# A 16 x 512-byte load on SP's queue ahead of the first large load of an Lp-pooling kernel

## The chip, the cores and the metric

The kernel runs on one core of a Trainium2 chip. The metric is the device time of one execution in microseconds; the number of record is the median of three runs. Profiles come from one execution of their own, recorded by the hardware profiler.

## The reference

The input x is float32, 32 x 256 x 4096; p is 2 and kernel_size is 4. Each output is the root of the mean of the squares of four neighbours:

```python
for i in range(out_length):                      # out_length = length // kernel_size
    start = i * kernel_size
    end = start + kernel_size
    window = np.abs(x[:, :, start:end]) ** p
    result[:, :, i] = (np.mean(window, axis=-1)) ** (1.0 / p)
```

So 134.2 MB are read, 33.6 MB are written, and each element is used once.

## The kernel before

x is taken as one flat array, and so is the output. The work is cut into 20 pieces, each of 128 partitions by up to 13,184 floats (52,736 bytes in a partition, 6.6 MB in all). Pieces form six blocks (L51): four of four pieces, then pieces 18, 16 and 17, then piece 19 alone. Within a block each partition holds one contiguous stretch of x.

There are three tiles for pieces of x, xt0 to xt2 (`X_SLOTS`, L43); piece i goes to tile i modulo 3. The tile `ot` holds four pieces' results, and a tile `st` in PSUM takes the sums of pieces 4, 8, 12 and 16. A tile `first` of one column serves a square root of a constant at the start (L129).

The steps of a piece:
- `load(i)` (L79 to L83): SP issues a DMA from x to the tile, in SP's queue.
- `square` (L88, L89): ACT squares the tile in place.
- `pairs` (L91 to L95) and `fours` (L97 to L99): DVE adds the squares in two steps, to a quarter of the length.
- `roots` (L106, with `root` in L102): ACT takes the square root with a scale of 1/4, for one piece or several neighbouring ones.
- `store(b, queue)` (L85, L86): a block of results goes out, blocks 0 to 2 from ACT's queue, blocks 3 to 5 from SP's.

The order is written by hand (`manual_schedule`, L62): each engine carries out its instructions in the order of the program text. Loads 0 to 2 are issued first (L122, L123). From then on load i + 3 is issued after the sums of piece i (L144, L145), since it overwrites the same tile; SP waits there for DVE. The last three pieces are treated apart (L147 to L172): DVE takes over part of the squares of pieces 18 and 19, and the last two blocks are stored separately.

Each DMA adds to a semaphore when it has landed. The DMAs of the program take eight such semaphores in turn.

The part that the change touches is the place just ahead of L122, before anything has been issued on SP, and the list of tiles in L58 to L61.

Of the kernel before, what the change touches and what calls it, by code (L numbers as in the profile page):

```python
# [1 line left out]

# [4 lines left out]


@with_exitstack
def kernel(  # L10
    ctx: ExitStack,
    tc: tile.TileContext,
    x: bass.AP,
    p: float,
    kernel_size: int,
    out: bass.AP,
):

    nc = tc.nc

    assert float(p) == 2.0, "kernel specialized for p == 2"
    k = int(kernel_size)  # L30
    assert k == 4, "kernel specialized for kernel_size == 4"

    P = nc.NUM_PARTITIONS
    fp32 = mybir.dt.float32
    Act = mybir.ActivationFunctionType
    add = mybir.AluOpType.add
    xf = x.rearrange("b c l -> (b c l)")
    of = out.rearrange("b c l -> (b c l)")
    total = xf.shape[0] // P

    W = 13184
    R = W // k
    X_SLOTS = 3  # L43
    NARROW = W - 32
    LAST = total - 18 * W - NARROW
    widths = [W] * 3 + [NARROW] + [W] * 15 + [LAST]
    n = len(widths)
    assert 0 < LAST <= W and LAST % 16 == 0


    blocks = [[0, 1, 2, 3], [4, 5, 6, 7], [8, 9, 10, 11], [12, 13, 14, 15], [18, 16, 17], [19]]  # L51
    block_of = {i: b for b, group in enumerate(blocks) for i in group}
    block_width = [sum(widths[i] for i in group) for group in blocks]

    x_pool = ctx.enter_context(tc.tile_pool(name="x_pool", bufs=1))
    o_pool = ctx.enter_context(tc.tile_pool(name="o_pool", bufs=1))
    s_pool = ctx.enter_context(tc.tile_pool(name="s_pool", bufs=1, space=bass.MemoryType.PSUM))
    x_tiles = [x_pool.tile([P, W], fp32, name=f"xt{j}") for j in range(X_SLOTS)]  # L58
    o_tile = o_pool.tile([P, 4 * R], fp32, name="ot")
    first = o_pool.tile([P, 1], fp32, name="first")  # L60
    s_tile = s_pool.tile([P, 4096], fp32, name="st")  # L61
    ctx.enter_context(tc.manual_schedule())  # L62

    def rows(flat, b, div):
        at = sum(block_width[:b]) * P // div
        return flat[at:at + block_width[b] * P // div].rearrange("(p w) -> p w", p=P)


    free = x_tiles[17 % X_SLOTS]
    place = {i: o_tile[:, i % 4 * R:i % 4 * R + widths[i] // k] for i in range(16)}  # L70
    place[18] = free[:, R:2 * R]
    place[19] = free[:, 0:LAST // k]
    place[16] = free[:, 2 * R:3 * R]
    place[17] = free[:, 3 * R:4 * R]
    held = [o_tile[:, 0:w // k] for w in block_width[:4]] + [free[:, R:4 * R], place[19]]

    xs, loads, stores, sums, squares = {}, {}, {}, {}, {}

    def load(i):  # L79
        b = block_of[i]  # L80
        at = sum(widths[j] for j in blocks[b][:blocks[b].index(i)])
        xs[i] = x_tiles[i % X_SLOTS][:, 0:widths[i]]
        loads[i] = nc.sync.dma_start(out=xs[i], in_=rows(xf, b, 1)[:, at:at + widths[i]])  # L83

    def store(b, queue):  # L85
        stores[b] = queue.dma_start(out=rows(of, b, k), in_=held[b])  # L86

    def square(v):  # L88
        return nc.scalar.activation(out=v, in_=v, func=Act.Square)  # L89

    def pairs(v):  # L91

        q = v.rearrange("p (n j) -> p n j", j=k)
        h = v[:, 0:v.shape[1] // 2].rearrange("p (n j) -> p n j", j=2)
        return nc.vector.tensor_tensor(out=h, in0=q[:, :, 0:2], in1=q[:, :, 2:4], op=add)  # L95

    def fours(o, v):  # L97
        h = v[:, 0:v.shape[1] // 2].rearrange("p (n j) -> p n j", j=2)
        return nc.vector.tensor_tensor(out=o, in0=h[:, :, 0], in1=h[:, :, 1], op=add)  # L99

    def root(o, s):
        return nc.scalar.activation(out=o, in_=s, func=Act.Sqrt, scale=1.0 / k)  # L102

    summed = {i: s_tile[:, 0:R] if i in (4, 8, 12, 16) else place[i] for i in range(n)}

    def roots(*group):  # L106
        if len(group) == 1:
            root(place[group[0]], summed[group[0]])
        else:
            v = o_tile[:, group[0] % 4 * R:(group[-1] % 4 + 1) * R]  # L110
            r = root(v, v)
            if group[0] in (5, 9):

                implied(r, stores[block_of[group[0]] - 1])
        if group[-1] in (3, 7, 11):
            store(block_of[group[-1]], nc.scalar)

    def implied(later, earlier):

        tc.declare_no_dep(later.ins, earlier.ins, reason="implied by the other waits")  # L120

    for i in range(X_SLOTS):  # L122
        load(i)  # L123


    ahead = {4: (3,), 8: (7,), 12: (11,)}
    behind = {3: [(0, 1, 2)], 7: [(5, 6), (4,)], 11: [(9, 10), (8,)], 14: [(12,)], 15: [(13, 14)], 16: [(15,)]}

    root(first[:, :], nc.const_aps.tensor(1.0, (P, 1), fp32))  # L129
    for i in range(17):  # L130
        if i in ahead:
            roots(*ahead[i])
        s = square(xs[i])
        squares[i] = s
        if i == 3:
            implied(s, squares[0])
        if i in (3, 7, 11):

            for earlier in sums[i - X_SLOTS]:
                implied(s, earlier)  # L140
        for group in behind.get(i, []):
            roots(*group)
        sums[i] = pairs(xs[i]), fours(summed[i], xs[i])
        if i + X_SLOTS < n:  # L144
            load(i + X_SLOTS)  # L145

    store(3, nc.sync)  # L147
    square(xs[17])
    pairs(xs[17])
    fours(summed[17], xs[17])  # L150
    later = {18: 4608, 19: 2000}

    def shared_square(i):
        v = xs[i][:, 0:later[i]]
        nc.vector.tensor_tensor(out=v, in0=v, in1=v, op=mybir.AluOpType.mult)  # L155
        square(xs[i][:, later[i]:widths[i]])

    def shared_pairs(i):
        implied(pairs(xs[i]), loads[i])

    shared_square(18)
    roots(16)
    roots(17)
    shared_pairs(18)
    fours(summed[18], xs[18])
    shared_square(19)
    roots(18)
    store(4, nc.sync)
    shared_pairs(19)
    fours(summed[19], xs[19])  # L170
    roots(19)
    store(5, nc.sync)  # L172


# [1 line left out]
_INS = ['x', 'p', 'kernel_size']  # L176
_OUTS = [((32, 256, 1024), 'float32')]

_NUMBERS = {'p': 2.0, 'kernel_size': 4}


# [26 lines left out]
```

## Time and profile before

| | |
|---|---|
| median of 3 runs | 394.06 us (393.84 to 394.38) |
| span of the profiled execution, first to last instruction | 392.3 us |
| median less that span | 1.8 us |
| ACT busy | 274.4 us (70%), 37 instructions |
| DVE busy | 218.2 us (56%), 42 instructions |
| GpSimd busy | 0.2 us, 4 instructions |
| HBM read and written | 134.22 MB and 33.55 MB |
| mean rate over the span | 428 GB/s |

Times inside the execution count from its first instruction. The profile names engines ACT (ScalarE), DVE (VectorE), POOL (GpSimd) and SP (SyncE); "SPq" is the issue of DMAs by SP and "ACTq" that by ACT. A row such as `xt<-in_x_dram` is what an instruction writes and reads, and L83 is a line of the kernel. A transfer is cut into packets, which 16 DMA engines carry; the packet records give the start, the duration and the size of each. The profiled execution's own time beyond its span isn't recorded; the median of the runs stands beside it.

### The profile page before, as it was taken

How to read it: one execution, taken by the hardware profiler on the slowest of the kernel's cores; microseconds unless marked ns; L12 is line 12 of the kernel's file. 1: busy time of each engine (PE TensorE's matmuls, PEld its weight loads, DVE VectorE, ACT ScalarE, POOL GpSimd, SP SyncE). 2: the span in 40 equal slices, each digit the busy share in tenths (PEclk: the TensorE clock that was granted, in tenths of full speed). 3: DMA queues.
4: the chain of work that ended last, by engine and by line, in shares of the span. 5: the costliest groups of instructions: out<-in, count | busy, mean ns of one | idle time of the engine just before them, and what ended most of it. 6: DMA issues, size and time to landing. Idle time of an engine off the chain costs nothing.

```text
span 392.3 us, 176 instructions
## 1 busy us (share of the span) xinstructions
DVE 218.2 (56%) x42; ACT 274.4 (70%) x37; POOL 0.2 (0%) x4
## 2 busy tenths in 40 slices
DVE  0009477580693274905942748069418485699970
ACT  1095695979950859799509597995098999969910
POOL 0000000000000000000000000000000000000000
DMA  8999999999999999999999999999999999999997
GB/s 344 430 430 430 430 440 435 452 457 366 430 430 430 430 430 430 430 441 446 452 446 441 436 430 436 430 430 430 430 430 430 430 430 430 430 453 415 430 413 342
DMA packets 3744, 167.77 MB, mean 428 GB/s; under 512 B 416, under 2 KB 416, under 8 KB 416
## 3 DMA queue, kind: packets, MB, share of 16 engines
q1 hardware_dynamic: 3312, 147.53, 87.4%
q10 hardware_dynamic: 432, 20.25, 11.9%
HBM read 134.22 MB, written 33.55 MB: 428 GB/s over the span
## 4 chain that ended last, share of the span: by engine, by line
DMA 43%; ACT 30%; DVE 23%; issue 0%; ACTq 0%; SPq 0%; DVEq 0%
DMA xt<-in_x_dram 43%; ACT xt L89 28%; DVE xt L95 14%; DVE ot L99 5%; DVE xt L99 3%; DVE xt L155 2%; ACT ot L102 2%; ACT xt L102 1%; ACTq L86 0%; SPq L83 0%; DVEq L95 0%
## 5 line engine op out<-in xcount | busy, mean ns | idle before, releaser
L89 ACT ACTIVATE xt<-xt 128x13184 f32<-128x13184 f32 (+3 forms) x20 | 216.7, 10847 | 92.3 <-DMA xt<-in_x_dram 91.0
L95 DVE TENSOR_TENSOR xt<-xt 128x6592 f32<-128x6592 f32 (+2 forms) x20 | 139.7, 6985 | 144.1 <-ACT xt L89 143.9
L99 DVE TENSOR_TENSOR ot<-xt 128x3296 f32<-128x3296 f32 (+1 forms) x13 | 46.7, 3592 | 17.9 <-DMA out_dram<-ot 17.6
L102 ACT ACTIVATE ot<-ot 128x6592 f32<-128x6592 f32 (+3 forms) x8 | 37.2, 4655 | 7.0 <-DVE ot L99 7.0
L102 ACT ACTIVATE xt<-xt 128x3296 f32<-128x3296 f32 (+1 forms) x3 | 8.5, 2836 | 8.8 <-DVE xt L99 8.8
L99 DVE TENSOR_TENSOR st<-xt 128x3296 f32<-128x3296 f32 x4 | 14.4, 3600 | 0.1
L99 DVE TENSOR_TENSOR xt<-xt 128x3296 f32<-128x3296 f32 (+1 forms) x3 | 10.4, 3461 | 0.1
L102 ACT ACTIVATE ot<-st 128x3296 f32<-128x3296 f32 x3 | 8.7, 2898 | 0.0
L155 DVE TENSOR_TENSOR xt<-xt 128x4608 f32<-128x4608 f32 (+1 forms) x2 | 7.2, 3593 | 0.0
L102 ACT ACTIVATE xt<-st 128x3296 f32<-128x3296 f32 x1 | 2.9, 2898 | 0.0
L102 ACT ACT_TABLE_LOAD x1 | 1.3, 1283 | 0.7 <-PEq L189 0.7
L102 ACT ACTIVATE first<-const-float32-1.0 128x1 f32<-128x1 f32 x1 | 0.2, 202 | 0.0
L189 POOL MEMSET const-bfloat16-1.0<- 128x1 bf16 x1 | 0.1, 101 | 0.0
L189 POOL MEMSET const-uint8-127<- 128x1 uint8 x1 | 0.1, 101 | 0.0
L189 POOL MEMSET const-float32-0.0<- 128x1 f32 x1 | 0.1, 98 | 0.2 <-issue 0.2
L189 POOL MEMSET const-float32-1.0<- 128x1 f32 x1 | 0.1, 98 | 0.0
## 6 DMA issues: line engine op xcount, KB each, us to landing
xt<-in_x_dram SPq DMA_DIRECT2D x18, 6592.0 KB, 29.8
out_dram<-ot ACTq DMA_DIRECT2D x2, 6592.0 KB, 35.1
out_dram<-ot SPq DMA_DIRECT2D x1, 6592.0 KB, 37.1
out_dram<-ot ACTq DMA_DIRECT2D x1, 6588.0 KB, 36.3
xt<-in_x_dram SPq DMA_DIRECT2D x1, 6576.0 KB, 24.7
xt<-in_x_dram SPq DMA_DIRECT2D x1, 5840.0 KB, 21.9
out_dram<-xt SPq DMA_DIRECT2D x1, 4944.0 KB, 16.1
out_dram<-xt SPq DMA_DIRECT2D x1, 1460.0 KB, 8.2
```

Source lines behind the costliest of these rows:

```text
L89: return nc.scalar.activation(out=v, in_=v, func=Act.Square)
L95: return nc.vector.tensor_tensor(out=h, in0=q[:, :, 0:2], in1=q[:, :, 2:4], op=add)
L99: return nc.vector.tensor_tensor(out=o, in0=h[:, :, 0], in1=h[:, :, 1], op=add)
L102: return nc.scalar.activation(out=o, in_=s, func=Act.Sqrt, scale=1.0 / k)
L155: nc.vector.tensor_tensor(out=v, in0=v, in1=v, op=mybir.AluOpType.mult)
L189: nc = _bacc.Bacc("TRN2", target_bir_lowering=False, num_devices=1)
```

## The change

One tile is added, 16 partitions of 128 floats, and one DMA into it, issued on SP ahead of the three large loads. Its source is x seen as 16 equal rows, of which the first 128 floats each are read; neighbouring rows are 8 MiB apart. Nothing in the kernel reads the tile.

```diff
     s_tile = s_pool.tile([P, 4096], fp32, name="st")
+    spare = o_pool.tile([16, 128], fp32, name="spare")
     ctx.enter_context(tc.manual_schedule())
...
+    nc.sync.dma_start(out=spare[:, :], in_=xf.rearrange("(p w) -> p w", p=16)[:, 0:128])
     for i in range(X_SLOTS):
         load(i)
```

## The prediction

> **What bounds the kernel now.** I read the busy table first: ACT 70% and DVE 56% busy, neither of them full. Then the slices and the DMA queues:
>
> ```profile
> span 392.3 us, 176 instructions
> DMA  8999999999999999999999999999999999999997
> GB/s 344 430 430 430 430 440 435 452 457 366 430 430 430 430 430 430 430 441 446 452 446 441 436 430 436 430 430 430 430 430 430 430 430 430 430 453 415 430 413 342
> DMA packets 3744, 167.77 MB, mean 428 GB/s; under 512 B 416, under 2 KB 416, under 8 KB 416
> q1 hardware_dynamic: 3312, 147.53, 87.4%
> q10 hardware_dynamic: 432, 20.25, 11.9%
> ```
>
> The DMA row is at 9 or more in every slice but the first (8) and the last (7), and the two queues together take 99.3% of the time of the 16 DMA engines. The reader is to see that the bytes are the bound: 167.77 MB at the 430 GB/s of most slices is 390.2 us of a span of 392.3. q1 is SP's queue (20 loads, three stores), q10 is ACT's (three stores). 3,744 packets are 26 transfers times 16 engines times 9, eight of data and one that counts the semaphore (the 416 small ones).
>
> Next, the queue's own waits and the times at which ACT gets its tiles:
>
> ```profile
> SPq L83 <- DVE ot L99: 239.4, 13, 38.6
> SPq L83 <- DVE st L99: 91.0, 4, 24.9
> ```
>
> ```profile
> 0.73 1.28 ACT L102 ACT_TABLE_LOAD   x1 [0.73 <-PEq L189]
> 2.02 0.20 ACT L102 ACTIVATE first<-const-float32-1.0 128x1 f32<-128x1 f32 x1
> 18.79 11.19 ACT L89 ACTIVATE xt<-xt 128x13184 f32<-128x13184 f32 x1 [16.56 <-DMA xt<-in_x_dram]
> 34.35 11.19 ACT L89 ACTIVATE xt<-xt 128x13184 f32<-128x13184 f32 x1 [4.38 <-DMA xt<-in_x_dram]
> 49.94 11.19 ACT L89 ACTIVATE xt<-xt 128x13184 f32<-128x13184 f32 x1 [4.39 <-DMA xt<-in_x_dram]
> 65.47 11.16 ACT L89 ACTIVATE xt<-xt 128x13152 f32<-128x13152 f32 x1 [4.34 <-DMA xt<-in_x_dram]
> ```
>
> SP's long waits for DVE (239.4 and 91.0 us) look like a bound and are not. They are waits to issue a load into a tile that is still in use, while the transfers issued before keep the rings full: load 3 goes out at 40.75 us and lands at 65.45, behind load 2, which lands only at 49.92. Loads arrive every 15.6 us (18.79, 34.35, 49.94, 65.47), and 15.6 is eight packets of 52,736 bytes at 1.947 us, the time of nearly every one in the packet records. So one transfer follows the other on each engine with nothing between. Counted packet by packet, fewer than 16 engines are busy for practically no time between 4 us and 388 us. At the end it is the same: store 5 is issued at 383.18 us and lands at 391.40, behind store 4 (landed at 387.90), itself behind store 3 (376.22). The spacing of the last two, 3.5 us, is 1.5 MB at 430 GB/s. The chain of waits credits ACT and DVE with the last 50 us, but the store it ends in still has about 4.7 us of earlier bytes ahead of it when it is issued.
>
> Hence the rule for this case: whatever shifts the start of the stream of packets shifts the end by the same amount; computing follows along. Only the first microseconds have to be worked out.
>
> **The start, before.** On SP's queue:
>
> ```profile
> 0.73 0.38 SPq L83 DMA_DIRECT2D xt<-in_x_dram  x1
> 1.16 0.42 SPq L83 DMA_DIRECT2D xt<-in_x_dram  x1
> 1.64 0.42 SPq L83 DMA_DIRECT2D xt<-in_x_dram  x1
> ```
>
> Load 0 is issued at 0.73 us; issues that follow each other directly are 0.43 and 0.48 apart. The first packets of load 0 start on the 16 engines between 1.74 and 2.49 us, 1.01 to 1.76 after the issue. They take 2.01 to 3.00 us, not 1.947, the ones that start first the longest, and all end between 4.34 and 4.81. From then on each packet takes 1.947. The first round thus carries an excess of 0.06 to 1.06 us an engine, 0.72 in the mean.
>
> **The change, part by part.**
> - *One more issue on SP, ahead of load 0.* It waits for nothing and stands where load 0 stood, at 0.73. Load 0 moves by one spacing: 0.43 from the first row (0.38 busy and 0.05 to the next). Bounds: the shortest issue, 0.33 with its 0.05 (later loads), gives 0.37; the longest spacing gives 0.48. I take 0.43. Loads 1 and 2 move as well, which costs nothing of its own: their packets queue behind load 0, whose first landing is near 18 us. Nobody else stands behind this on SP; load 3 is issued 40 us in.
> - *Its own packets.* 16 rows of 512 bytes: I take one row for each engine, and a semaphore packet. At the pace of the large packets 512 bytes are 0.019 us, a semaphore packet takes 0.009: 0.028 an engine. If one engine had to carry all 16 rows it would be 16 x 0.019 = 0.31 on that one. I take 0.03.
> - *The excess of the first round.* It is the unknown. Whatever delays the first packets may be paid again by load 0 (change 0), or once only, by the tiny load, beside load 0's issue. At best every first packet of load 0 starts at 1.74 + 0.43 = 2.17 and takes 1.947: the round ends at 4.12, not 4.80, which is 0.68 *earlier* than before in spite of the added issue. With the old spread of starts but no excess, the last engine ends at 2.49 + 0.43 + 1.95 = 4.87, a loss of 0.07. At worst the tiny load is paid in full ahead of load 0 (below, +1.46). Of rows near it: on q10, store 0's first packets, the first on that ring, take 1.946 with no excess, but there the engines were already streaming. No record shows a small load ahead of a large one on idle engines. The nearest row is load 0 itself, issued on idle engines, and load 0 would still be the first large transfer; I take the excess as paid again.
> - *The semaphore.* The DMAs take eight semaphores in turn, and a transfer waits for the one eight before it on the same semaphore. All shift by one, so the pairs stay as they are; load 6 alone gets a new partner, the tiny load, done some 85 us earlier. Nothing, or 0.02 (the length of a semaphore wait that is already satisfied). At the end SP waits for the same eight semaphores; another order among them could move 0.03 to 0.1 us.
> - *The spare tile.* 512 bytes in each of 16 partitions; nothing reads it, and no engine instruction is added.
>
> Sum: 0.43 + 0.03 + 0 = 0.46 us. The profiled span goes from 392.3 to 392.8. The median of the runs, 394.06, is 1.8 us over the span (work before the first and after the last instruction, which the edit leaves alone), so 394.06 + 0.46 = 394.5. The three runs before spread over 0.54 us, as much as the effect.
>
> **Rivals.**
> - *Absorbed.* The tiny load takes the excess upon itself while load 0 is being issued. For it: engines that start later have less excess (start 1.74: 2.87 us; start 2.49: 2.01 us), as if something became ready near 2.4 to 2.8 us, whatever had started before. Against it: that readiness may belong to each transfer that meets idle engines. It gives -0.68 to +0.1, so 393.4 to 394.2, most likely near 394.0.
> - *Slower: the tiny load completes before load 0 begins.* If an idle ring finishes a one-packet transfer, up to its semaphore, before it takes up the next, load 0's first packets wait for that landing. Load 0's fixed part is 18.77 - 0.73 - 15.58 = 2.46 us, so the tiny load would land near 0.73 + 2.46 = 3.2, and load 0's early engines would start then in place of 1.74: +1.46, so 395.5 if the excess is paid again too. It passes the 0.2% from a start of 2.53 us on. Against it: loads 0 and 1 follow each other with no gap, 15.6 us to 15.6 of packets; the semaphore packet of load 0 holds an engine for 0.009 us and is counted some 0.35 us later while load 1 already runs. That speaks for rings that run on, but a stall could hide in eight long packets more easily than behind one short one.
> - *It does nothing:* the load is dropped since nothing reads the tile. Then 394.06. Nothing in the diff drops it, and one packet more per engine would be visible.
>
> On the slower rival, the Trainium skill, "DMA: Bandwidth & Descriptors", section "Anatomy of one DMA", gives each transfer a fixed cost of about 2.0 us, most of it the wait until the last byte is confirmed, and measures that on GpSimd's path, not on SP's. Taken as a serial cost it would make the sum 394.06 + 2.0 = 396.1, an estimate from that page. The trace has 2.46 us for load 0, which met idle engines, and none for loads 1 to 3, which were queued behind others; so the fixed part overlaps where the ring is full, and what it does behind a tiny load no row shows.
>
> **How the numbers follow.** Chances: paid again (394.3 to 394.7) 0.50; absorbed (393.4 to 394.2) 0.32; serial (395.2 to 395.5) 0.10; nothing 0.02; something not thought of 0.06. The prediction is the first: 394.5. The range runs from the lower bound of the unknown excess, 393.4, to 395.1, the forecast with its bounds and the spread of the runs; most of the serial case is left out. A measurement of this kernel can tell about 0.2%, 0.8 us, from no change. The first two cases and the idle one lie within that (0.84); slower by more is the serial case and a little of the unknown (0.12); for faster by more no mechanism is seen, since the start has 0.68 to give at most (0.04).
>
> **What the profile after would show.** One issue more in SP's queue, and 3,776 packets (one of data and one for the semaphore on each of 16 engines, 32 more). Load 0 issued at 1.16; its first packets starting at 2.2 to 2.9, and ending at 4.8 to 5.3 (paid again), at 4.1 to 4.9 (absorbed) or near 6 (serial). ACT's first square at 19.2, 18.8 or 20.2. All later loads 15.6 apart, landings shifted by one and the same amount to the end. The prediction is wrong in its ground if the shift at the first square is not the shift at the end: then the stream has slack that I did not see, or the order of packets of the two queues has changed.

## The result and the profile after

The changed kernel takes 394.71 us (median of 18 runs, 394.58 to 395.06) against 394.06 (18 runs, 393.82 to 394.49). The ratio is 1.0017, with a 95% interval of 1.0010 to 1.0023: 0.4 to 0.9 us slower, clear of noise, and inside the prediction's 0.2% by its middle (0.17%). The mean of the runs moved by 0.71 us, the profiled span by 0.72 (392.26 to 392.98).

The page of the changed kernel, first the span, the slices and the queues:

```profile
span 393.0 us, 177 instructions
DMA  8999999999999999999999999999999999999997
DMA packets 3776, 167.78 MB, mean 427 GB/s; under 512 B 432, under 2 KB 448, under 8 KB 448
q1 hardware_dynamic: 3344, 147.54, 87.2%
q10 hardware_dynamic: 432, 20.25, 11.9%
```

There is one instruction more and there are 32 packets more, as the change says, and the stream is as full as before. SP's issues at the start, from the timeline:

```profile
0.73 0.38 SPq L123 DMA_DIRECT2D spare<-in_x_dram  x1
1.16 0.41 SPq L84 DMA_DIRECT2D xt<-in_x_dram  x1
1.62 0.42 SPq L84 DMA_DIRECT2D xt<-in_x_dram  x1
```

The tiny load is issued where load 0 was, and load 0 at 1.16 in place of 0.73. ACT's squares show when the loads arrive:

```profile
19.77 11.19 ACT L90 ACTIVATE xt<-xt 128x13184 f32<-128x13184 f32 x1 [17.55 <-DMA xt<-in_x_dram]
35.35 11.19 ACT L90 ACTIVATE xt<-xt 128x13184 f32<-128x13184 f32 x1 [4.39 <-DMA xt<-in_x_dram]
50.95 11.19 ACT L90 ACTIVATE xt<-xt 128x13184 f32<-128x13184 f32 x1 [4.40 <-DMA xt<-in_x_dram]
66.46 11.17 ACT L90 ACTIVATE xt<-xt 128x13152 f32<-128x13152 f32 x1 [4.33 <-DMA xt<-in_x_dram]
```

These are later by 0.98, 1.00, 1.01 and 0.99 us, more than twice what load 0's issue moved. The packet and landing records of the two profiles, side by side (us; each of the 16 engines reports its share of a transfer as landed, and the table has the first, the last or the mean of the 16):

```
                                          before          after           shift
load 0 issued                             0.729           1.163           0.43
load 0, first packets end: mean           4.60            5.10            0.50
load 0, first packets end: last engine    4.81            5.76            0.96
load 0 landing, first / last engine       18.29 / 18.77   18.69 / 19.75   0.41 / 0.98
load 0 landing, mean of the engines       18.56           19.07           0.50
load 4 landing, last engine               81.03           82.04           1.00
load 7 landing, last engine               144.38          145.06          0.68
load 17 landing, last engine              331.22          331.93          0.71
load 17 landing, mean of the engines      330.86          331.37          0.52
last landing (store 5), last engine       391.40          392.06          0.66
last landing (store 5), mean              391.01          391.53          0.52
end of the span                           392.26          392.98          0.72
```

In the mean of the 16 engines the stream is later by the same amount at the first load and at the last store, 0.50 and 0.52 us. Two things differ from a plain shift. The engines' first packets end over 1.01 us instead of 0.46, and a square waits for the last engine's landing, so it shows 0.98. The last engine's shift falls from 1.00 to 0.64 between the landings of load 4 (82 us) and load 5 (102 us), where the first store runs beside the loads. From load 4 to load 7 the last engine's distance from the mean grows from 0.18 to 0.39 us in the kernel before and shrinks from 0.69 to 0.56 in the changed one; the mean's shift stays. And the end of the span moves by 0.06 more than the last landing.

That 0.06 comes from SP's last instructions. SP waits for the eight semaphores in four pairs, some 0.065 us each once they are reached. Before, store 5's semaphore is in the third pair, so one pair follows the last landing and the kernel ends 0.855 us after it. One DMA more shifts the turn of the semaphores: store 5's is in the second pair, two follow, and the end comes 0.917 us after the last landing.

### The profile page after: what moved, and what is told of

It is laid out like the page before. It is cut to its first block, busy times and chain, and to the rows that moved or that the text cites. A ratio compares the mean times of both kernels' runs of the same rounds, so it can differ in the third digit from the quotient of the medians.

```text
span 393.0 us, 177 instructions
## 1 busy us (share of the span) xinstructions
DVE 218.2 (56%) x42; ACT 274.4 (70%) x37; POOL 0.2 (0%) x4
## 4 chain that ended last, share of the span: by engine, by line
DMA 43%; ACT 30%; DVE 23%; issue 0%; ACTq 0%; SPq 0%; DVEq 0%
DMA xt<-in_x_dram 43%; ACT xt L90 28%; DVE xt L96 14%; DVE ot L100 5%; DVE xt L100 3%; DVE xt L157 2%; ACT ot L103 2%; ACT xt L103 1%; ACTq L87 0%; SPq L123 0%; SPq L84 0%; DVEq L96 0%
```

## The experiments

My theory, A: load 0's issue is displaced by one issue spacing (the time from one issue to the next), and the stream carries that to the end one to one. The rivals: the transfer itself costs, wherever it stands; the tiny load's packets or their far-apart rows cost; the slow first packets (a cold start) are paid once. Times before in these comparisons are 394.02 to 394.11. Spans are known for every run, so the table after the experiments uses the mean span against that of the kernel before on the same chip.

**The tiny load behind load 0.**

```diff
-    nc.sync.dma_start(out=spare[:, :], in_=xf...[:, 0:128])
     for i in range(X_SLOTS):
         load(i)
+        if i == 0:
+            nc.sync.dma_start(out=spare[:, :], in_=xf...[:, 0:128])
```

> The same tiny load, issued on SP behind load 0 instead of ahead of it; all else as in the changed kernel. Theory A (the displaced issue): the cost is load 0's later start, so load 0 is issued at 0.73 again, its first round ends at 4.3 to 4.8, and the median is within 0.15 us of before (394.06). Rival B (the extra transfer itself, wherever it stands: its packets, one more turn of the eight semaphores, the longer wait at the end): the median stays near 394.7. The part of the end that hangs on the order of the last semaphore waits (0.06 us in the profile of the changed kernel) should stay by both.

394.05 us, ratio 1.0000 (0.9992 to 1.0009), as theory A has it. The issues in its timeline:

```profile
0.73 0.38 SPq L84 DMA_DIRECT2D xt<-in_x_dram  x1
1.16 0.42 SPq L126 DMA_DIRECT2D spare<-in_x_dram  x1
1.63 1.13 SPq L84 DMA_DIRECT2D xt<-in_x_dram  x2
```

Loads 1 and 2 are issued as late as in the changed kernel, and nothing is lost: their packets queue behind load 0. Only the place ahead of load 0 costs. The end still comes 0.917 us after the last landing, and the mean span is 0.06 longer with an error of 0.05: that 0.06 of the end, and no more.

**The tiny load from ACT's queue.** `nc.sync` becomes `nc.scalar` in the added line.

> The same tiny load, issued from ACT's queue at the start, where it stands ahead of nothing but a table load and a root of a constant. In the traces of before and after, every engine loses about 1.0 us near 92 us, at the first packets of ACT's queue (store 0), and nothing at stores 1 and 2. Theory A for the start (displaced issue) expects no loss there, load 0 issued at 0.73. On the stall at 92 us: if it belongs to the first use of a ring, the tiny load takes it at the start, partly hidden, and the median falls by up to 1.0 us, to 393.1 to 393.9; if it belongs to the first write to the output, the stall stays and the median is 394.0 to 394.2. If the tiny load's packets disturb load 0's first round as much as they do from SP, 394.4 to 394.7.

394.08 us, ratio 1.0001 (0.9992 to 1.0010): again nothing is lost. A second thing was tried here. In the profile of the kernel before, each engine's packet in progress at 92 us, shortly after store 0 is issued, takes about 3 us in place of 1.95, a loss of 1.00 us an engine. It stays here (0.70), so it is not the first use of ACT's queue; the kernel with the tiny load behind load 0, which leaves that queue alone, has 0.72.

**Two tiny loads.**

```diff
+    spare2 = o_pool.tile([16, 128], fp32, name="spare2")
...
+    nc.sync.dma_start(out=spare2[:, :], in_=xf...[:, 128:256])
```

> Two tiny loads on SP ahead of load 0 (the second takes the next 512 bytes of each row into a tile of its own). Theory A: one more issue spacing, 0.43 to 0.46, so load 0 issued at 1.6 and the median at 395.1 to 395.3, 1.1 above before. A rival by which the first load pays once (a cold start, widened spread of the engines) and the second is free: 394.7 to 394.8.

395.22 us, ratio 1.0027 (1.0016 to 1.0039). Load 0 is issued at 1.62, 0.89 later, and the mean span is 1.19 longer. Load 0's first packets still take 2.04 to 3.17 us, so two tiny loads do not take the cold start upon themselves either:

```profile
0.73 0.38 SPq L124 DMA_DIRECT2D spare<-in_x_dram  x1
1.16 0.41 SPq L125 DMA_DIRECT2D spare<-in_x_dram  x1
1.62 1.36 SPq L85 DMA_DIRECT2D xt<-in_x_dram  x3
```

**One row only.**

```diff
-    nc.sync.dma_start(out=spare[:, :], in_=xf...[:, 0:128])
+    nc.sync.dma_start(out=spare[0:1, :], in_=xf...[0:1, 0:128])
```

> The tiny load cut to one row of 512 bytes, at the same place on SP. The issue stays, but I expect packets on one engine only. Theory A (displaced issue alone): load 0 issued at 1.16 and +0.43 in the mean, 394.4 to 394.6. If the rest of the measured 0.65 comes from handing the small packets out engine by engine (the spread of the first round's ends grew from 0.46 to 1.01 us), the spread falls back to about 0.5 and the median to about 394.5; if the spread was chance of one profile, it and the median stay at 394.7.

394.50 us, ratio 1.0010 (1.0001 to 1.0019). The records show one data packet of 0.025 us and one semaphore packet. Load 0 is issued 0.39 later (this issue is shorter, 0.33):

```profile
0.73 0.33 SPq L123 DMA_DIRECT2D spare<-in_x_dram  x1
1.12 1.30 SPq L84 DMA_DIRECT2D xt<-in_x_dram  x3
```

The mean span is 0.45 longer: 0.39 and the 0.06 of the end, with nothing left over. The spread of the first round's ends did not fall to 0.5 as expected. It was 0.74 in this profile, and with no tiny load ahead of load 0 it is anything from 0.45 to 0.91, so one profile's spread is not a safe reading.

**Rows side by side.** The source becomes `xf[0:2048]` in 16 rows of 128.

> The tiny load at its place ahead of load 0 on SP, its 16 rows now side by side in x (8,192 bytes in one piece) instead of 8 MiB apart. In the changed kernel's trace its packets lengthen from 0.025 to 0.345 us an engine, the late ones most. Theory A (issue displaced by 0.43, the packets handed to the engines some 0.05 us apart, and late ones meeting load 0's first packets): distance plays no part, the first round's ends spread over about 1 us as in the changed kernel, and the median is 394.6 to 394.8. Rival (rows a large power of two apart are slow to read): the packets take 0.025 us, the first round ends some 0.1 to 0.3 us earlier on the last engines, and the median is 394.4 to 394.55.

394.56 us, ratio 1.0018 (1.0009 to 1.0027). The packets all take 0.025 us, as the rival said. But the time doesn't decide: of 11 runs eight lie at 394.3 to 394.8 and three at 395.1 to 395.5, the median is 0.5 and the mean 0.7 above before. Whether the distance of the rows matters stays open.

**128 rows.** The spare tile gets 128 partitions, and the source 128 rows of 512 bytes.

> The tiny load with 128 rows of 512 bytes instead of 16, into a spare tile of 128 partitions: the same single issue, eight data packets on each engine. Theory A: the issue spacing stays at 0.43 to 0.46 and sets most of the cost; the packets add 8 x 0.025 = 0.2 us an engine at most, part of it while load 0 is being issued: 394.6 to 394.9. Rival (the cost is the bytes and packets, eight times as many): +0.2 of what the small load costs beyond its issue becomes +1.6, so 396. If a full set of small packets takes the excess of load 0's first round upon itself, 394.3 to 394.5.

395.04 us, ratio 1.0026 (1.0016 to 1.0036), a little over what A allowed.

```profile
0.72 0.37 SPq L123 DMA_DIRECT2D spare<-in_x_dram  x1
1.15 1.37 SPq L84 DMA_DIRECT2D xt<-in_x_dram  x3
```

The issue is the same (load 0 at 1.15), so the packets do cost: load 0's first packets end 1.32 us later in the mean, over 1.97 us, and its last engine lands 1.87 later. And yet the last landing is only 0.81 later. In the mean of the engines the landing is 1.40 later at load 0 and 0.66 at the last one. What was given back shows near 92 us, where each engine loses 0.20 us in place of 1.00.

**A tiny store at the start, from ACT, and from SP behind load 2.** No load; DVE fills the tile with zeros first.

```diff
     for i in range(X_SLOTS):
         load(i)
+    nc.vector.memset(spare[:, :], 0.0)
+    nc.scalar.dma_start(out=of.rearrange("(p w) -> p w", p=16)[:, 0:128], in_=spare[:, :])
```

(The second one has `nc.sync` in the last line.)

> No tiny load. Instead DVE fills the spare tile with zeros and ACT stores it at the start, 16 rows of 512 bytes into the output (rows that stores 0 to 5 overwrite later). It tests the one-time loss of about 1.0 us an engine near 92 us, at store 0's first packets, which the tiny load on ACT left in place. If the loss belongs to the first write to the output, or to the first transfer of that kind on ACT's queue, the tiny store takes it at the start, where SP's stream runs on: loss at 92 us under 0.3 us, median down by up to 0.9, to 393.1 to 393.7. If the loss belongs to the change from reading alone to reading and writing in a full stream, it stays: 393.9 to 394.2.

> As the tiny store from ACT, but issued on SP behind loads 0 to 2, so that its packets pass about 49 us in. If the first write to the output is what costs 1.0 us near 92 us, the loss goes (or moves to 49 us, if it stops all engines there as well: no gain then, 394.0). If it needs ACT's queue, the loss at 92 us stays and the median is 394.0 to 394.2.

Both take 394.40 us, ratio 1.0009 (1.0001 to 1.0018), above what was expected of either. The loss near 92 us stays (0.98 and 0.90), so it is not the first write to the output either. The spans hardly moved (0.12 and 0.07 longer, of which 0.06 is the end): another 0.28 lies outside the span. It came back in each kernel with a fill on DVE.

**Load 0 held back without any tiny load.**

```diff
+    nc.vector.memset(x_tiles[0][:, 0:400], 0.0)
     for i in range(X_SLOTS):
         load(i)
```

> No tiny load at all. DVE writes zeros to the first 400 columns of load 0's tile ahead of it, so that SP waits for DVE before it issues load 0 (DVE is otherwise idle until 30 us). By the 0.28 us that ACT waited for a 128-column fill in an earlier run, load 0 should be issued 0.35 to 0.55 later. Theory A (the issue's displacement is the cost): the first round's ends move by that in the mean, with no wider spread than before (0.46), the profile's span by 0.3 to 0.6, the median to 394.4 to 394.6. Rival (the delay of load 0 is taken up by slack, and the tiny load's packets are the cost): 394.0 to 394.1. The runs with a tiny store showed medians 0.36 above before with hardly any change of span, and both had a fill on DVE: if such a fill costs 0.36 outside the span, this median is 394.8.

> The same with 4,000 columns, so that load 0 is issued 1.2 to 4.3 us later. Theory A: the end moves by as much as the issue, one to one (0.85 to 1.15 of it), in the span and in the median; the difference between this and the short delay is free of any constant cost of the fill. Rival (the start has slack, or the stretch near 92 us gives late starts back): less than half of the delay reaches the end.

394.92 us (ratio 1.0021, 1.0012 to 1.0030) and, with 4,000 columns, 398.74 us (1.0119, 1.0105 to 1.0133). The two timelines, the short delay first:

```profile
0.88 0.39 DVE L122 MEMSET xt<- 128x400 f32 x1 [0.88 <-PEq L190]
1.29 1.32 SPq L83 DMA_DIRECT2D xt<-in_x_dram  x3
```

```profile
1.63 3.39 DVE L122 MEMSET xt<- 128x4000 f32 x1 [1.63 <-PEq L190]
5.05 1.32 SPq L83 DMA_DIRECT2D xt<-in_x_dram  x3
```

SP issues load 0 as soon as the fill has ended. The issue moves by 0.57 and 4.32 us; the mean spans by 0.58 and 4.38. From the one to the other the issue moves by 3.76, the median by 3.82: one to one, free of what a fill costs outside the span. This is the price of a displaced first load, measured by itself. The short delay's median lies 0.3 above the range that theory A gave it, by about that constant 0.28; the expectation had named such a cost of the fill as possible.

**128 rows from ACT's queue.**

> The 128-row tiny load issued from ACT's queue at the start, so that SP's load 0 keeps its place. With 128 rows on SP the loss near 92 us shrank from 1.0 to 0.2 us an engine. If that was because the load touches all of x, 1 MiB apart, ahead of time (or engages each engine fully), the loss stays small here while load 0 is issued at 0.73: first round 0.1 to 0.3 late in the mean, median 393.4 to 393.8, faster than both kernels. If it shrank because the engines had spread over 1.9 us by then, the loss is back at 0.7 to 1.0 unless the spread is there too, and the median is 394.1 to 394.5.

394.32 us, ratio 1.0009 (1.0000 to 1.0018). Not the gain hoped for: the loss near 92 us is back at 0.77, with load 0's first round spread over 0.45 us. That the load touches x ahead of time is refuted as the reason for the 0.20 seen with SP. The mean span is 0.29 longer, though load 0 keeps its place. Eight packets of 0.025 to 0.027 us on each engine are 0.2 us of a full stream, about what is left over beside the 0.06 of the end.

**The tiny load, and load 0 held back until its packets have passed.** The changed kernel with the fill of 1,300 columns ahead of the loop.

> The tiny load as in the changed kernel, and besides it a fill of 1,300 columns on DVE that holds load 0 back until about 2.2 us, when the tiny load's packets have all passed (in the changed kernel the last of them start at 2.69 us, and load 0's first at 2.20 already). Of the changed kernel's mean span, 0.74 above before over its runs, 0.43 is the issue and 0.06 the end; 0.25 is left over. If the rest comes from the overlap of the tiny load's late packets with load 0's first round (engines held up), it goes: mean span above before by the issue's shift plus 0.06 plus at most 0.1. If the rest is the price of the packets themselves or of something else that the tiny load brings, it stays: the shift plus 0.3. The median is 0.28 more than the span says, as with every fill on DVE.

396.02 us, ratio 1.0049 (1.0035 to 1.0062).

```profile
0.73 0.39 SPq L123 DMA_DIRECT2D spare<-in_x_dram  x1
1.07 1.14 DVE L124 MEMSET xt<- 128x1300 f32 x1 [1.07 <-PEq L192]
2.24 1.30 SPq L84 DMA_DIRECT2D xt<-in_x_dram  x3
```

The issue of load 0 moves by 1.51, the mean span by 1.61. With the end's 0.06, 0.04 us is left over, with an error of 0.09; the changed kernel has 0.21 by its own runs, with an error of 0.05: 0.71 less 0.43 and 0.06 (the 0.74 and 0.25 of the expectation took other runs of before). This points to a rest that goes when the two transfers don't meet at the start, but the difference, 0.17, is less than twice its error of 0.10, so it isn't shown. The records fit: here all 16 packets take 0.025 us; in the changed kernel they take 0.025 to 0.065 until load 0's first packets start (2.20 us), and up to 0.345 after that.

All in one table, us against the kernel before. "Left over" is what remains of the mean span's growth without the two columns ahead of it. The error of a mean is 0.04 to 0.07, 0.1 for two tiny loads and the last row, 0.13 for rows side by side; for the change itself the mean of the runs stands in place of the mean span.

| kernel | load 0 issued later | end after last landing later | mean span longer | left over |
|---|---|---|---|---|
| the change | 0.43 | 0.06 | 0.71 | 0.21 |
| behind load 0 | 0 | 0.06 | 0.06 | 0.00 |
| from ACT | 0 | 0.06 | 0.05 | -0.01 |
| two tiny loads | 0.89 | 0.13 | 1.19 | 0.16 |
| one row | 0.39 | 0.06 | 0.45 | 0.00 |
| rows side by side | 0.45 | 0.06 | 0.72 | 0.21 |
| 128 rows | 0.42 | 0.06 | 1.03 | 0.55 |
| tiny store from ACT | 0 | 0.06 | 0.12 | 0.05 |
| tiny store from SP | 0 | 0.06 | 0.07 | 0.01 |
| held back, 400 columns | 0.57 | 0 | 0.58 | 0.02 |
| held back, 4,000 columns | 4.32 | 0 | 4.38 | 0.06 |
| 128 rows from ACT | 0 | 0.06 | 0.29 | 0.23 |
| tiny load, then held back | 1.51 | 0.06 | 1.61 | 0.04 |

## Why the prediction was right

*The time.* 394.71 us is 0.65 above before by the medians and 0.71 by the means, against 0.46 forecast. It lies at the upper edge of what "paid again" was given (394.3 to 394.7). All 18 runs (394.58 to 395.06) lie above the "absorbed" case and below the serial one.

*The bound.* Right. A later start reaches the end one to one, shown by the two delays (3.76 us of issue, 3.82 us of time). One kernel is an exception: with 128 rows half of the late start came back near 92 us. The prediction counted busy engines there and did not see that their packets are slow: it names store 0's first packets, 1.946 us with no excess, but the load packets just ahead of them take 2.6 to 3.1.

*The sign of being wrong that it named.* It came: the shift at the first square, 0.98, is not the shift at the end, 0.72. The prediction left out that a square waits for the last of 16 engines, and so moves with their spread as well. In the mean of the engines the shift is 0.50 at load 0 and 0.52 at the last landing, so the ground held, and the sign was badly chosen. Its other half, another order of the two queues' packets, came where store 0 runs: load 5's mean landing is 0.33 earlier and load 6's 1.37 later than before, and load 7's is 0.49 later again.

*The issue, 0.43 us.* Right to the hundredth (0.729 to 1.163), and it is the largest part. Behind load 0, or from ACT, the same load costs no more than the 0.06 of the end.

*Its own packets, 0.03 us.* The term that was mis-sized: 0.21 us is left over by the runs. 0.025 us a packet is what they take where nothing runs beside them; what happens where they meet load 0 was not in the sum. The tiny load is handed to the engines one after the other, its packets start 1.74 to 2.69 us, some 0.05 apart. On four of the later engines load 0's first packet starts at 2.70 to 2.90, right behind the tiny load's semaphore packet. Load 0's first packets end 0.50 us later in the mean, and the last of them 0.96; that one starts early, at 2.30, and takes 3.47 us, where the longest in the kernel before took 3.00. In the two profiles the stream's mean is 0.09 later than the issue explains, and at the last landing the last engine is 0.53 behind the mean in place of 0.39. The latter is 0.22 to 0.54 in the fourteen profiles, so this pair alone can't tell chance from the change. What is left over grows with the rows (0.00 with one, 0.21 with 16, 0.55 with 128, of which 0.2 is the bare time of eight packets an engine), and with one tiny load that has passed before load 0 comes it is 0.04. That the meeting of the two transfers is the cause is thus likely and not shown, and how the engines hold each other up there is open.

*The excess of the first round, taken as paid again.* Right in its effect: the first packets still take 1.9 to 3.5 us, and their mean end moves by the issue and 0.07. The rival "absorbed" is refuted by this and by two tiny loads, whose load 0 has 0.77 of excess in the mean, against 0.72 before. A plain delay has the excess too (0.76 with 400 columns).

*The semaphores.* Nothing in the loop, as said; the 0.03 to 0.1 allowed for another order at the end is 0.06, and was left out of the sum.

*The slower rival.* Refuted: load 0's first packets start at 2.20 us, and the tiny load lands between 2.10 and 3.18. With 128 rows three engines start load 0 at 2.20, 2.23 and 2.41, before any engine's share of the tiny load has landed (2.49). So an engine goes on to load 0 without waiting for that landing. The Trainium skill, "DMA: Bandwidth & Descriptors", section "Anatomy of one DMA", gives a fixed cost of about 2.0 us for each DMA on GpSimd's path; on SP's queue the runs here show 0.71 us for the whole change, so that cost can't be added serially here.

By the runs the parts are 0.43 for the issue, 0.06 for the end and 0.21 left over. The last is a remainder, so that they add up to 0.71 proves nothing about it.

## What to carry to other kernels

Where the DMA engines are full from the first transfer to the last, as here, look at the first large load's issue: it is on the path that sets the end. A DMA put ahead of it on its queue cost its issue spacing (0.43 us) and, with 16 rows, some 0.2 us more. The same DMA behind that load, or from ACT's queue, cost at most 0.06 us. A landing waits for the last of 16 engines: compare the mean of the engines before you conclude that a stream has slack. Warming up a queue with a small transfer bought nothing here: the slow first packets came again.

## What was not expected of the hardware

- Between 92 and 95 us, 1.5 to 3 us after store 0 is issued beside the loads, each engine's packet in progress takes about 3 us in place of 1.95. That loses 1.0 us an engine in the kernel before and in the changed one, once, and not at stores 1 and 2. In thirteen of the fourteen kernels the loss is 0.70 to 1.02. It nearly went (0.20) in the one in which the engines had been spread over 1.97 us at the start, a whole packet's time; that matches what came back of that kernel's late start. Its cause is open; that it strikes engines which switch to the store all at once is only a guess.
- A fill as DVE's first instruction lengthened the time by 0.28 us outside the span (2.05 to 2.07 us outside it instead of 1.78, in all five kernels with a fill, from 128 to 4,000 columns). A span alone would have hidden it. Why is open.
- The number of DMAs in the program sets which of SP's last waits comes after the last landing, and so 0.06 us of the end: 0.855 us with 26, 0.917 with 27, 0.986 with 28.
